# One-hot marks of the expert gates: per-token instructions with scalars in place of broadcast products

## The chip, the cores and the metric

The kernel runs on one core of a Trainium2 chip, as one launch. The metric is the device time of that launch in microseconds (us), here the median of several executions. TensorE multiplies matrices, VectorE (DVE) and ScalarE (ACT) work element by element, GpSimd (POOL) issues the gathers by index, and SyncE (SP) issues most other transfers.

## The reference, cut to what matters

The model is two layers over 512 latent tokens with 256 context tokens before them. Each layer has four token mixers and then a product-key expert layer (PEER), which alone matters here. For every token and each of 8 heads, 16 of the 128 x 128 experts are chosen, so 128 in all; expert (i, j) has a row of the table U and a row of the table V:

```python
top_s, top_j = lax.top_k(cand, PEER_TOPK)
eidx = jnp.take_along_axis(cidx, top_j, axis=-1)
gate = jax.nn.softmax(top_s, axis=-1)
act = jax.nn.gelu(jnp.einsum('td,thkd->thk', xb, u_tab[eidx]).astype(F32))
return jnp.einsum('thk,thkd->td', (gate * act).astype(xb.dtype), v_tab[eidx])
```

## The kernel before, in words

The function `peer` runs once per layer. Most tokens are handled densely: U's products are taken for all 16,384 experts and later multiplied by a gate that is zero wherever a token did not choose the expert. The last tokens (256 in layer 0, 128 in layer 1) gather their chosen rows instead. That leaves 512 dense tokens in layer 0 and 384 in layer 1.

Several streams of work run side by side:

- `s_part` takes U in 128 blocks. ScalarE rounds a block to its high half (`uh`, line 250), VectorE subtracts to get the low half (`ul`, line 251), and TensorE makes 24 long products (`d.S`) from the halves. Both halves have two buffers. `s_ahead(n)` lays n such blocks out at a given place.
- `choose` uses gathered rows on VectorE (lines 1500 and 244, 1024 elements each), copies the next indices (line 1522) and lets GpSimd issue the next gathers (line 1527).
- `route` finds a tile's experts (128 tokens) on VectorE, with long runs of short instructions.
- `build` makes the dense gates of a tile. It transposes the tile's row, column and gate, so that a partition holds one of the 128 choices and the columns are tokens (`ijT`). For a token, a mark for the row is a vector of 128 numbers per choice, one at the row's place and zero elsewhere; likewise for the column. The product of the row marks (weights) with the column marks times the gate, summed over the choices on TensorE, is the 128 x 128 matrix of that token's gates. The gate is split into two fp16 parts, so there are two matmuls per token, into the same PSUM place. ScalarE copies the result out for four tokens at a time.

`build` goes in blocks of 32 tokens: first `s_ahead(5)` in layer 0 or `s_ahead(3)` in layer 1, then twice 16 tokens: marks, `choose` (1 row per block in layer 0, 6 in layer 1), matmuls, copies; then a block goes to DRAM. In layer 0 each block of U also calls `choose` for two rows. The tile framework arranges the instructions of each engine by the order of the program and by what is ready in its planned times, so the streams come out interleaved; each engine then runs its own list in that order.

In the trace, the row marks (`o1`) lie in memory of the residual stream and are named `ro.x`, the column marks are `rt.o`, their products with the gate parts `rt.og`, and the gate matmuls `rt.k<-rt.og,ro.x`. Small helpers record every operation, so many have the helper's line: 236 for a product of two tensors, 240 and 241 for one with scalars, 254 for a matmul.

Before, four tokens at a time lie side by side in `o1`, `o2` and `og` (the innermost step runs over tokens), and a matmul reads every fourth element:

```python
tt(o1, i4, col(0), A.is_equal)
ins = tt(o2, i4, col(1), A.is_equal)
for i in range(2):
    tt(og[:, i], o2, col(2 + i), A.mult)
```

Of the kernel before, what the change touches and what calls it, by code (L numbers as in the profile page):

```python
# [26 lines left out]
# ---------------------------------------------------------------- layout on the host  # L27
# [90 lines left out]
def consts():  # L118
    o = {}
    for n, L in (("l", SEQ), ("c", CTX)):  # L120
        # Half of the times and of the frequencies: e and o below are the sums and differences of the tokens t and
        # their mirror images, of which the even and the odd frequencies need one each for cosine and sine.
        # 0: the filters, t against L - t; 1, 2: tokens, t + 1/2 against L - t - 1/2, and back.
# [91 lines left out]
# ---------------------------------------------------------------- the program  # L215

def body(tc, I, out, dbg=None, stop=None):
# [56 lines left out]
    def segs(n):  # L274
        """columns in PSUM banks: the latents' 512, then the context's 256 before them"""
        return [(max(0, n - 512), n)] + ([(0, n - 512)] if n > 512 else [])

    with pool("keep") as kp, pool("scr", space=DRAM) as dp:
        # ---------------------------------------------------------- persistent
# [13 lines left out]
        def inv_sqrt(o, i, scale, eps_ap_or_val):  # L293
            """(i * scale + eps) ** -0.5"""
            act(o, i, AF.Ln, scale, eps_ap_or_val)
            act(o, o, AF.Exp, -0.5)
# [10 lines left out]
        # ---------------------------------------------------------- modulation vectors  # L307
        def ada(l, rounds, wp, pp, cs, dma, bufs):
            """columns 2048 * r on; the two vectors' products lie on partitions 32 * q and 32 * q + 1"""
# [23 lines left out]
        # ---------------------------------------------------------- Hyena's filters  # L333
        def dft_part(p, n, L, kind, f):
            """two parts each of the cosines and sines of 128 frequencies"""
            t = T(p, [128, 2, 2, L // 2], F32R, "dft", 2)
            G.dma_start(t, I["dft_" + n][:, kind, f])
            if kind < 2:
                t = t.rearrange("p a b (j m) -> p a b j m", m=128)
            return (t[:, 0, 0], t[:, 0, 1]), (t[:, 1, 0], t[:, 1, 1])  # L340

        def sin_(p, t, ps, frq, bias, L):
            """sin(frq * (ps + bias)) with the argument brought to [-pi, pi]"""
# [13 lines left out]
        def spectrum(l, n, L, p, pp, dst_):  # L357
# [12 lines left out]
            # the first half of the times on the upper partitions; the second, mirrored and with the middle in the  # L370
            # place of time L, on the lower ones
# [10 lines left out]
            # forward plus and minus backward, each the sum (0) and difference (1) of a time and its mirror image  # L382
# [34 lines left out]
            # 1 / (L * (sum of the absolute values + EPS)); 1/L = 2/N is the weight of a frequency in the inverse  # L417
# [5 lines left out]
            for f in range(NC):  # L423
# [15 lines left out]
                if f == 0:  # L439
                    # the highest frequency, in the place of the sine of frequency 0  # L440
# [16 lines left out]
        # ---------------------------------------------------------- prologue  # L457
# [18 lines left out]
        # ---------------------------------------------------------- shared pieces  # L476
        def rms_scale(p, pp, srcs, n, tag, tags=(("sq", 2), ("rstd", 1))):
            """1 / sqrt(mean of squares over all rows + EPS), on every partition"""
# [14 lines left out]
        def norm_mod(hps, p, pp, x, l, which, t0, tag, cut=None):  # L493
            """what the products read, in two parts; for the tokens before and from cut on in a pool each"""
# [16 lines left out]
        def projector(wp, pp, src, tag, off=0, ks=range(8), eng=None):  # L511
            """rows of a product with h for the tokens from t0 on, by segments; early(c) fetches a row's weights"""
# [26 lines left out]
        def padded(p, zd, c, tag, bufs, t0):  # L539
            """a row block of z with two zeros before and one behind each stream, in three stretches of 256 tokens"""  # L540
# [12 lines left out]
        def conv(o, xp, taps, bias, t0):  # L553
            """o = sum of w * (token + shift) + bias; the first tap carries the bias"""
# [26 lines left out]
        # ---------------------------------------------------------- RG-LRU  # L581
# [68 lines left out]
        # ---------------------------------------------------------- RWKV-7  # L650
# [5 lines left out]
        def rwkv_prep(l, zd, t0, pp, p):  # L656
            """what the recurrences read, for both tiles of channels; the long parts go through DRAM"""
# [25 lines left out]
            for c in range(2):  # L683
# [6 lines left out]
                # -- decays, keys and the like, channels on partitions  # L690
# [72 lines left out]
                # -- the masked products N whose (1 - N)^-1 each chunk needs; the inverses of their diagonal blocks  # L763
                # of 16, row by row, with a block on each partition
# [27 lines left out]
                # the gate g: what the read-out multiplies by and adds  # L792
# [26 lines left out]
        def rwkv_load(l, st, p):  # L819
            """what all chunks read"""  # L820
# [15 lines left out]
        def rwkv_chain(l, c, t0, stt_, y, p, pp, qp):  # L836
            """the chunks of 128 tokens of one tile of channels, both directions side by side, as generators that can be
            laid out alternately: the inverses of a chunk, and its recurrence"""
# [10 lines left out]
            def inverse(step):  # L849
# [7 lines left out]
                # Wm[d, s]: C against A and R, B against A and R, with the tokens' order as a mask  # L857
# [11 lines left out]
                # XZ[g, d]: the inverse of direction d where g != d, its transpose where g == d  # L869
# [91 lines left out]
        def rwkv_out(l, t0, n, stt_, y, p, pp, tag):  # L961
            """the read-out of the chunks n of both tiles, normed as a group"""
# [34 lines left out]
        def alternate(*gens):  # L997
            """lays the generators' pieces out in turn; (n, g) begins n rounds later"""
# [6 lines left out]
        # ---------------------------------------------------------- mLSTM  # L1005
        def colmajor(ap, t0):
            """the latents' columns of a token row, walked (row, col) where they lie (col, row)"""
            return ap.rearrange("p (c r) -> p r c", r=8)
# [184 lines left out]
        # ---------------------------------------------------------- Hyena  # L1193
        def mix_hyena(l, n, zd, ydst, p, pp):
# [16 lines left out]
            for o in range(2):  # L1211
                # sums (0) and differences (1) of the tokens and their mirror images
# [13 lines left out]
                for f in range(NC):  # L1226
# [9 lines left out]
                    # the sine part of the transform is -q[:, 1]  # L1236
# [12 lines left out]
                # what the tokens and their mirror images have in common (0), and half their difference (1)  # L1249
# [22 lines left out]
        # ---------------------------------------------------------- the four mixers  # L1272
# [6 lines left out]
        def mixers(l, xin):  # L1279
            """xin: (pool, tile) of the residual stream"""  # L1280
# [134 lines left out]
        # ---------------------------------------------------------- PEER  # L1415
        def peer(l, xin):
# [5 lines left out]
            # the last tokens gather the rows that they chose; the others' products go over all rows  # L1422
# [21 lines left out]
            # x waits in DRAM while the routing uses its place  # L1444
# [3 lines left out]
            spare = [xf[:, NE * GB + i * n1:NE * GB + i * n1 + n1].bitcast(F16).rearrange("p (a b c) -> p a b c", a=4, b=128)  # L1448
# [18 lines left out]
            def s_ahead(n):  # L1467
                """U's products, which don't wait for the routing"""
# [9 lines left out]
            def token_rows(t):  # L1478
                """h of a tile of tokens, a token on each partition"""
# [12 lines left out]
            # the last tokens' experts, tile by tile: row e of U, later of V for every token; what has come is used at  # L1492
            # the next calls
# [39 lines left out]
            # ---- routing  # L1533
# [7 lines left out]
            def scores(hc, piece):  # L1541
                """the 16 best keys of half a head for the tokens of a piece"""
# [21 lines left out]
            def route(p, t, io16):  # L1564
                """a tile's experts, of the 16 x 16 pairs of every head the 16 best, and their gates"""
                svh = sv[:, t].rearrange("p (h c) k -> p h c k", c=2)
                # a pair (a, b) with (a + 1)(b + 1) > 16 has 16 before it that are no less: 4 x 16 and 12 x 4 pairs do
# [16 lines left out]
                # the places in the two lists  # L1584
# [13 lines left out]
                # and the keys there  # L1598
# [30 lines left out]
            if CUT[l]:  # L1629
                # the gathered tokens first: their rows come in beside all that follows  # L1630
# [25 lines left out]
            with pool("rg", side=far) as p:  # L1656
                # whole numbers, each four times over: DVE's 2-byte mode needs neighbours in every operand
                iota = T(p, [128, 128, 4], BF, "iota")
                G.dma_start(iota, I["iota"])
                ioth = T(p, [128, 128, 4], F16, "ioth")  # L1660
                V.tensor_copy(ioth, iota)
                i4 = ioth[:, None].broadcast_to((128, 4, 128, 4))
# [3 lines left out]
                def build(t, f):  # L1666
                    """the gates of the tokens of a tile, for all experts"""
# [3 lines left out]
                    # row and column as fp16 whole numbers; the gate, at most 1, times 2^14 as two fp16 parts  # L1671
                    ijT = T(p, [128, 4, 128], F16, "ijT", 2)
                    S.copy(ijT[:, 0:2], ps[:, 0:2])
                    gr = T(p, [128, 128], F32, "gr", 2)
                    act(gr, ps[:, 2], AF.Copy, 2.0 ** 14)
                    V.tensor_copy(ijT[:, 2], gr)
                    tt(ijT[:, 3], gr, ijT[:, 2], A.subtract)
                    for b in range(128 // GB):
# [5 lines left out]
                        for t16 in range(0, GB, 16):  # L1684
                            tk = slice(b * GB + t16, b * GB + t16 + 16)
                            col = lambda i: ijT[:, i, tk].rearrange("p (b t) -> p b t", t=4)[:, :, None].broadcast_to((128, 4, 128, 4))
                            o1 = spare[t16 // 16 % 2]
                            o2 = T(p, [128, 4, 128, 4], F16, "o2", 1)
                            og = T(p, [128, 2, 4, 128, 4], F16, "og", 2)
                            tt(o1, i4, col(0), A.is_equal)  # L1690
                            ins = tt(o2, i4, col(1), A.is_equal)
                            for i in range(2):
                                tt(og[:, i], o2, col(2 + i), A.mult)
# [151 lines left out]
```

## Time and profile before

| | us |
|---|---|
| median of 3 runs | 4990.23 |
| lowest and highest run | 4975.98, 4994.22 |
| profiled execution, span from first to last instruction | 5021.4 |
| TensorE busy in it | 4590.8 |
| VectorE busy in it | 3624.9 |
| ScalarE busy in it | 1777.9 |
| GpSimd busy in it | 1375.8 |

The profile is of one execution; its span stands beside the time of the runs, which are taken without a profile. A busy time is the time in which an engine has an instruction in work, and the start-to-start distance of two instructions can be shorter than the duration of one, since their beginnings and ends overlap. A wait names the instruction that ended last before the waiting one could start.

### The profile page before, as it was taken

The page shows a single profiled execution, that of the slowest core. Times are in us where ns is not written, and L with a number is a line of the kernel's source. Part 1 is how long each engine was busy: PE and PEld are TensorE (multiplying, and loading weights), DVE is VectorE, ACT ScalarE, POOL GpSimd, SP SyncE. Part 2 cuts the span into 40 slices and gives each one's busy share as a digit, 9 for nine tenths or more (in the row PEclk, how much of TensorE's full clock was granted, in tenths as well). Part 3 has the DMA queues.
Part 4 walks back from the last instruction along what each step waited for, and adds up shares of the span by engine and source line. Part 5 has one row for each costly group of instructions (what it writes and reads, how often), then busy time and mean ns, then how long its engine had stood idle before and what let it go on. Part 6 is the DMA issues. An engine that isn't in the chain of part 4 may idle for free. (4 is left out here: it accounts for less than half of the span.)

```text
span 5021.4 us, 66832 instructions
## 1 busy us (share of the span) xinstructions
PE 4590.8 (91%) x24203; PEld 3842.1 (77%) x24203; DVE 3624.9 (72%) x7303; ACT 1777.9 (35%) x2546; POOL 1375.8 (27%) x1117
## 2 busy tenths in 40 slices
PE   7879898799899999799999887898899998999998
PEld 3658567688777888687788665787688898999997
DVE  5772647399788897688889677556589875567777
ACT  4352222353233444322222335212534443333333
POOL 1211111002344454234455222000002332323332
PEclk9889999899999999899999898968999999999999
DMA  4442545346688999899999544203426889888896
GB/s 177 160 137 77 189 161 158 143 130 236 225 298 307 322 329 332 311 352 353 362 379 381 178 152 134 68 19 110 140 80 231 269 284 345 286 283 325 321 328 248
DMA packets 521083, 1170.01 MB, mean 233 GB/s; under 512 B 68192, under 2 KB 250272, under 8 KB 516272
## 3 DMA queue, kind: packets, MB, share of 16 engines
q1 hardware_dynamic: 227440, 563.42, 32.5%
q0 software_dynamic: 134912, 484.06, 27.2%
q10 hardware_dynamic: 158400, 118.25, 7.3%
q8 instruction: 191, 3.13, 0.3%
q14 instruction: 140, 1.15, 0.1%
HBM read 992.95 MB, written 173.02 MB: 232 GB/s over the span
## 5 line engine op out<-in xcount | busy, mean ns | idle before, releaser
L254 PE MATMUL d.S<-mrg.hhi,d.ul 128*128 128x512 f32 (+1 forms) x2048 | 772.6, 377 | 85.4 <-DVE d.ul L251 76.2
L1527 POOL DMA_INDIRECT d.grow<-in_V_dram,d.at x369 | 578.7, 1568 | 712.2 <-DVE d.at L1522 562.4
L254 PE MATMUL d.S<-mrg.hlo,d.uh 128*128 128x512 f32 (+1 forms) x2048 | 760.2, 371 | 0.1
L254 PE MATMUL d.S<-mrg.hhi,d.uh 128*128 128x512 f32 (+1 forms) x2048 | 757.6, 370 | 0.0
L254 PE MATMUL rt.O<-rt.pv,rt.pv 128*128 128x512 f32 (+1 forms) x2580 | 558.6, 366 | 41.5 <-DVE rt.pv L251 41.0
L254 PEld LDWEIGHTS rt.O<-rt.pv,rt.pv 128*128 128x128 f32 x2580 | 468.3, 189 | 108.8 <-issue 48.9
L254 PEld LDWEIGHTS d.S<-mrg.hhi,d.ul 128*128 128x128 f32 x2048 | 398.1, 194 | 144.5 <-DVE d.ul L251 94.7
L247 ACT ACTIVATE d.pa<-d.S 128x512 f32<-128x512 f32 (+1 forms) x256 | 139.7, 546 | 859.3 <-PE d.S L254 794.3
L254 PEld LDWEIGHTS d.S<-mrg.hlo,d.uh 128*128 128x128 f32 x2048 | 397.8, 194 | 39.2 <-DVE mrg.hlo L251 1.2
L254 PEld LDWEIGHTS d.S<-mrg.hhi,d.uh 128*128 128x128 f32 x2048 | 396.1, 193 | 41.4
L1527 POOL DMA_INDIRECT d.grow<-in_Ur_dram,d.at x233 | 302.9, 1300 | 433.2 <-DVE d.at L1522 326.8
L251 DVE TENSOR_TENSOR d.ul<-d.ur,d.uh 128x1024 fp32r<-128x1024 f32 x256 | 311.6, 1219 | 131.0 <-ACT d.uh L250 130.6
L1527 POOL DMA_INDIRECT rt.grow<-in_Ur_dram,rt.at x151 | 228.8, 1515 | 630.1 <-DVE rt.at L1522 569.4
L250 ACT CAST rt.pv<-rt.vr 128x1024 fp32r<-128x1024 f32 x172 | 181.1, 1053 | 588.0 <-DMA rt.vr<-in_V_dram 249.0
L1500 DVE SCALAR_TENSOR_TENSOR d.grow<-d.grow,rt.tok 128x1024 f32<-128x1024 f32 x233 | 281.9, 1221 | 121.6 <-DMA d.grow<-in_Ur_dram,d.at 120.8
L244 DVE SCALAR_TENSOR_TENSOR d.tok<-d.grow,rt.gw,d.tok 128x1024 f32<-128x1024 f32 x245 | 313.7, 1281 | 51.8 <-DMA d.grow<-in_V_dram,d.at 51.5
L254 PE MATMUL d.O<-rt.pv,rt.pv 128*128 128x512 f32 (+1 forms) x1548 | 337.5, 362 | 0.0
L254 PEld LDWEIGHTS d.O<-rt.pv,rt.pv 128*128 128x128 f32 x1548 | 280.7, 188 | 30.2
L254 PE MATMUL rt.O<-d.pv,d.pv 128*128 128x512 f32 (+1 forms) x1260 | 273.1, 365 | 8.1 <-DVE d.pv L251 7.2
L250 ACT CAST d.uh<-d.ur 128x1024 fp32r<-128x1024 f32 x256 | 267.5, 1046 | 27.7 <-issue 11.5
L254 PEld LDWEIGHTS rt.O<-d.pv,d.pv 128*128 128x128 f32 x1260 | 226.8, 188 | 44.1 <-issue 13.6
L254 PE MATMUL z.z<-hhi,z.wlo 128*128 128x512 f32 (+1 forms) x656 | 236.1, 360 | 23.5 <-POOL z.wlo L251 16.3
(619 smaller groups left out, 9380.0 us busy)
## 6 DMA issues: line engine op xcount, KB each, us to landing
d.ur<-in_U_dram SPq DMA_DIRECT2D x256, 512.0 KB, 5.2
rt.vr<-in_V_dram SPq DMA_DIRECT2D x256, 512.0 KB, 6.0
ada.adaw<-in_ada_w_dram POOLq DMA_DIRECT2D x80, 512.0 KB, 4.1
mrg.Ad<-d.pa ACTq DMA_DIRECT2D x128, 256.0 KB, 5.5
rt.gt<-mrg.Gd SPq DMA_DIRECT2D x32, 1024.0 KB, 9.4
rt.ga<-mrg.Ad SPq DMA_DIRECT2D x128, 256.0 KB, 6.9
mrg.Gd<-ro.x ACTq DMA_DIRECT2D x14, 2048.0 KB, 12.1
mrg.Gd<-rt.gst ACTq DMA_DIRECT2D x14, 2048.0 KB, 14.4
```

The lines of the kernel that those rows point to most:

```text
L244: return V.scalar_tensor_tensor(o, a, s, b, op0=op0, op1=op1)
L247: return S.activation(o, i, f, bias=bias, scale=scale)
L250: S.copy(hi, src)
L251: return (eng or V).tensor_tensor(lo, src, hi.bitcast(F32), op=A.subtract)
L254: PE.matmul(ps, l, r, start=start, stop=stop)
L1500: V.scalar_tensor_tensor(g, g, 1.0, s["h"], A.mult, A.mult, accum_out=w[:, e:e + 1])
L1527: G.indirect_dma_start(out=g, out_offset=None, in_=I["Ur"] if r % 256 < 128 else I["V"].rearrange("l j i d -> (l j i) d"), in_offset=bass. ...
```

## The change

For each token, one instruction makes the row marks by comparing 0 to 127 with the token's row, given as a per-partition scalar. Two more compare with the column and multiply by a part of the gate, both as per-partition scalars. The tile `o2` and one of the two buffers of `ijT` go away; `ijT` becomes fp32, as the scalars are read from it; the high part of the gate takes an extra cast. The 128 marks of a token now lie in a row, and the matmuls read them so. (The file's comments are also blanked, which changes no instruction.)

```diff
-            spare = [xf[...].bitcast(F16).rearrange("p (a b c) -> p a b c", a=4, b=128)
+            spare = [xf[...].bitcast(F16).rearrange("p (a b) -> p a b", b=128)
...
-                ioth = T(p, [128, 128, 4], F16, "ioth")
-                V.tensor_copy(ioth, iota)
-                i4 = ioth[:, None].broadcast_to((128, 4, 128, 4))
+                ioth = T(p, [128, 128], F16, "ioth")
+                V.tensor_copy(ioth, iota[:, :, 0])
...
-                    ijT = T(p, [128, 4, 128], F16, "ijT", 2)
+                    ijT = T(p, [128, 4, 128], F32, "ijT", 1)
                     S.copy(ijT[:, 0:2], ps[:, 0:2])
-                    gr = T(p, [128, 128], F32, "gr", 2)
-                    act(gr, ps[:, 2], AF.Copy, 2.0 ** 14)
+                    act(ijT[:, 3], ps[:, 2], AF.Copy, 2.0 ** 14)
+                    gr = T(p, [128, 128], F16, "gr", 2)
+                    V.tensor_copy(gr, ijT[:, 3])
                     V.tensor_copy(ijT[:, 2], gr)
-                    tt(ijT[:, 3], gr, ijT[:, 2], A.subtract)
+                    tt(ijT[:, 3], ijT[:, 3], ijT[:, 2], A.subtract)
...
-                            col = lambda i: ijT[:, i, tk].rearrange("p (b t) -> p b t", t=4)[:, :, None].broadcast_to((128, 4, 128, 4))
                             o1 = spare[t16 // 16 % 2]
-                            o2 = T(p, [128, 4, 128, 4], F16, "o2", 1)
-                            og = T(p, [128, 2, 4, 128, 4], F16, "og", 2)
-                            tt(o1, i4, col(0), A.is_equal)
-                            ins = tt(o2, i4, col(1), A.is_equal)
-                            for i in range(2):
-                                tt(og[:, i], o2, col(2 + i), A.mult)
+                            og = T(p, [128, 16, 2, 128], F16, "og", 2)
+                            for q in range(16):
+                                col = lambda i: ijT[:, i, tk][:, q:q + 1]
+                                ts(o1[:, q], ioth, col(0), None, A.is_equal)
+                                for i in range(2):
+                                    ins = ts(og[:, q, i], ioth, col(1), col(2 + i), A.is_equal, A.mult)
...
-                                        mm(pg[:, q4], o1[:, t4, :, q4], og[:, i, t4, :, q4], i == 1, i == 0)
+                                        mm(pg[:, q4], o1[:, 4 * t4 + q4], og[:, 4 * t4 + q4, i], i == 1, i == 0)
```

## Rows read from the trace of the kernel before

**Rows 1.** The page: its first line, and each engine's busy time.
```profile
span 5021.4 us, 66832 instructions
...
PE 4590.8 (91%) x24203; PEld 3842.1 (77%) x24203; DVE 3624.9 (72%) x7303; ACT 1777.9 (35%) x2546; POOL 1375.8 (27%) x1117
```

**Rows 2.** VectorE's groups by shape: count, busy us, mean ns, idle before.
```profile
L236 DVE TENSOR_TENSOR rt.og<-rt.o,rt.ijT 128x2048 f16<-128x2048 f16 x112 | 133.1, 1217 | 0.1
...
L236 DVE TENSOR_TENSOR ro.x<-rt.ioth,rt.ijT 128x2048 f16<-128x2048 f16 x56 | 68.2, 1218 | 9.5 <-PE rt.k L254 9.5
```

**Rows 3.** Busy time by engine in two stretches, clock, DMA share, GB/s.
```profile
1420.00:2064.00 644.00, 618.18 (x3168) 516.08 (x3166) 549.30 (x850) 273.00 (x323) 294.46 (x194) 0.98 0.92 315
3815.00:4142.00 327.00, 302.21 (x1856) 293.97 (x1855) 268.65 (x397) 157.41 (x191) 109.30 (x69) 0.92 0.84 280
```

**Rows 4.** The same for the gate parts alone: makers (DVE), users (PE).
```profile
1420.00:2064.00 644.00, 127.78 (x1024) 76.00 (x64) 0.98 0.92 315
3815.00:4142.00 327.00, 91.98 (x727) 57.06 (x48) 0.92 0.84 280
```

**Rows 5.** What VectorE waited for, 1420 to 2064: us, times, longest.
```profile
DVE d.ul L251 <- ACT d.uh L250: 30.2, 18, 6.6
DVE d.grow L1500 <- DMA d.grow<-in_Ur_dram,d.at: 26.8, 20, 4.6
DVE d.tok L244 <- DMA d.grow<-in_V_dram,d.at: 21.8, 22, 3.8
```

**Rows 6.** The same from 3815 to 4142.
```profile
DVE d.ul L251 <- ACT d.uh L250: 49.6, 27, 11.1
DVE ro.x L236 <- PE rt.k L254: 8.5, 9, 2.2
```

**Rows 7.** VectorE's timeline (start, us, instruction): a row's and column's marks.
```profile
3843.31 1.22 DVE L236 TENSOR_TENSOR ro.x<-rt.ioth,rt.ijT 128x2048 f16<-128x2048 f16 x1
3844.45 1.22 DVE L236 TENSOR_TENSOR rt.o<-rt.ioth,rt.ijT 128x2048 f16<-128x2048 f16 x1
```

**Rows 8.** The same timeline: 128 two-byte elements and a constant, twice.
```profile
1112.22 0.19 DVE L240 TENSOR_SCALAR rt.pf<-rt.pf 128x128 bf16<-128x128 bf16 x1
1112.33 0.49 DVE L1597 COPY_PREDICATED rt.pf<-rt.over,rt.pf 128x128 bf16<-128x128 uint8 x2
...
3952.54 0.18 DVE L240 TENSOR_SCALAR rt.pf<-rt.pf 128x128 bf16<-128x128 bf16 x1
3952.64 0.48 DVE L1597 COPY_PREDICATED rt.pf<-rt.over,rt.pf 128x128 bf16<-128x128 uint8 x2
```

**Rows 9.** The same: 128 fp32 elements, one per-partition scalar, and the next.
```profile
369.45 0.28 DVE L240 TENSOR_SCALAR rw.fs<-lru.sig,rp.fm 128x128 f32<-128x128 f32 x1
369.64 0.68 DVE L236 TENSOR_TENSOR rw.Wm<-rw.r,lru.msk 128x512 f32<-128x512 f32 x1
```

**Rows 10.** The same: two per-partition scalars at 184.86, constants at 186.64.
```profile
184.86 0.67 DVE L241 TENSOR_SCALAR rp.kd<-rp.ra,rp.rwpar 128x768 f32<-128x768 f32 x1
185.45 0.41 DVE L737 TENSOR_TENSOR_SCAN rp.cum<-cst,rp.lw__234_1169 128x128 f32<-128x128 f32 x1
...
186.64 0.55 DVE L241 TENSOR_SCALAR rp.ra<-rp.ra 128x768 f32<-128x768 f32 x1
187.11 1.68 DVE L737 TENSOR_TENSOR_SCAN rp.cum<-cst,rp.lw__234_1169 128x128 f32<-128x128 f32 x5
```

**Rows 11.** Instructions on rt.ijT: ns min/median/max, first and last start.
```profile
L1673 ACT CAST rt.ijT<-rt.k x7: 363/365/376, 1419.7 to 4046.8; 128x256 f16<-128x256 f32 x7
...
L236 DVE TENSOR_TENSOR rt.ijT<-rt.gr,rt.ijT x7: 277/281/284, 1423.2 to 4049.5; 128x128 f16<-128x128 f32 x7
```

**Rows 12.** TensorE's timeline: long products of 384 columns.
```profile
3842.82 0.33 PE L254 MATMUL d.S<-mrg.hhi,d.uh 128*128 128x384 f32 x1
...
3843.34 0.33 PE L254 MATMUL d.S<-mrg.hhi,d.uh 128*128 128x384 f32 x1
```

**Rows 13.** Line 240: ns min/median/max, first and last start.
```profile
L240 DVE TENSOR_SCALAR rt.pf<-rt.pf x10: 178/184/383, 1112.2 to 3952.5; 128x128 bf16<-128x128 bf16 x10
```

More of the change, by code (lines that the diff above doesn't have):

```diff
@@ L1447, in peer @@
             n1 = 4 * 128 * 4 // 2
-            spare = [xf[:, NE * GB + i * n1:NE * GB + i * n1 + n1].bitcast(F16).rearrange("p (a b c) -> p a b c", a=4, b=128)
+            spare = [xf[:, NE * GB + i * n1:NE * GB + i * n1 + n1].bitcast(F16).rearrange("p (a b) -> p a b", b=128)
                      for i in range(2)]
```

## The prediction

> **What bounds the kernel now.** I read the page first, for the shares of the engines over the span [rows 1]: TensorE is busy 91% and VectorE 72%. An average like this decides nothing for a change that touches one stage, so the second view is the list of VectorE's groups by line and shape. It shows what the marks are now: large fp16 tensor_tensors of 2048 elements, four for each 16 tokens, and 56 times 16 tokens in all [rows 2].
>
> The third view is the busy time of the engines in the two stretches in which the marks are made [rows 3]. In layer 0 (1420 to 2064 us) VectorE is busy 549.3 of 644 us and TensorE 618.2; in layer 1 (3815 to 4142 us) it is 268.7 and 302.2 of 327 us. The reader is to see that TensorE leads in both, and that VectorE has only 94.7 and 58.4 us free. The same windows for the gate parts alone give the split of the work: 64 of their instructions in layer 0 and 48 in layer 1, which is 32 and 24 times 16 tokens [rows 4].
>
> The fourth view says what VectorE's free time is made of. In layer 0, 30.2 us of it wait for ScalarE's rounded half of a U block (ScalarE there waits for TensorE to give a buffer back), and most of the rest for gathered rows to land [rows 5]. In layer 1, 49.6 us are of the first kind and 8.5 us wait for TensorE to free a mark buffer [rows 6]. So VectorE is second in both stretches by a small margin; in some stalls it is TensorE that waits for it.
>
> **What the change removes.** Four tensor_tensors for each 16 tokens. Each lasts 1.22 us, but the next begins before it ends: from start to start it is 1.14 us [rows 7]. So 4 x 1.14 = 4.56 us go.
>
> **What it adds.** For each token one tensor_scalar of 128 fp16 elements with one per-partition scalar, and two with two of them: 48 instructions for 16 tokens. No row has this form, so I build it from three neighbours, always from start to start.
> - A tensor_scalar of 128 two-byte elements with a constant is followed after 0.11 and 0.10 us, 0.105 in the mean [rows 8].
> - What a per-partition scalar costs: over 768 fp32 elements, the form with two of them is followed after 0.59 us, the one with constants after 0.47 us [rows 10]. That is 0.12 us for two, 0.06 for one.
> - A check: 128 fp32 elements with one per-partition scalar are followed after 0.19 us [rows 9]; fp32 streams more slowly, so this lies above 0.105 + 0.06 = 0.165, as it should.
>
> So the row's mark costs 0.165 us, a column mark with its gate part 0.105 + 0.12 = 0.225 us, a token 0.165 + 2 x 0.225 = 0.615 us, and 16 tokens 9.84 us. The change adds 9.84 - 4.56 = 5.28 us of VectorE for each 16 tokens: 169 us in layer 0 (32 times), 127 us in layer 1 (24 times), 296 us together. The ends: if the scalars cost nothing, 48 x 0.105 = 5.04 us and +0.48 (27 us in all); if fp16 ran only like the fp32 row, 0.19 and 0.25 us, then 11.04 us and +6.48 (363 us). I take 5.28, because its nearest rows have the element size and, apart, the scalars.
>
> **Where it lands.** VectorE would need 549.3 + 169 = 718 us in a stretch of 644, and 268.7 + 127 = 396 in one of 327. Cover for it is only the free time, so at least 74 and 69 us stick out, 143 together, and at most all 296. VectorE becomes the bound of both stretches. What stands behind the marks on its queue is the U blocks' low halves, which TensorE's long products wait for, and the gathered rows' products, after which the next gather is issued; all of them are late by as much. The products after the marks' stretch start when the gates are done, and none of the later work is moved into it. Of the free time I count as used up only the waits for ScalarE's half, 30.2 + 49.6 = 80 us: they come from TensorE holding a buffer, and end once VectorE is the late one. The waits for gathered rows stay, as the gathers are issued from the same queue of steps. That gives 296 - 80 = +216 us.
>
> **Small parts.** The row, column and gate tile becomes fp32 with one buffer in place of two. So the copies of the next tile of tokens wait for the last marks of the one before. From the first of these copies to the end of the last is 4 us (1419.7 to 1423.2 + 0.28) in layer 0 [rows 11]; at the five changes of tile that is 0 to 20 us, and I take 0, since routing, U blocks and gathered rows stand ready for VectorE there. The extra cast per tile is one of 7. The matmuls now read their marks in a row instead of every fourth element. 1,751 of the 1,792 fall into the two windows and keep TensorE 127.8 + 92.0 us, some 0.125 us each [rows 4]. The long products move 384 columns every 0.173 us (three steps in 0.52 us), 0.058 us per 128 [rows 12]. So the layout may give between 0 and 1,792 x 0.067 = 120 us of TensorE. On the path I take 0, because TensorE no longer ends these stretches.
>
> **The sum.** The profiled execution spans 5021.4 us; the median of the runs is 4990.2, 0.6% less. 5021 + 216 = 5237 us for a profiled span, and at the same ratio (0.9938) 5205 us for the median. The bounds +143 and +296 give 5132 and 5284.
>
> **Rivals.**
> - *The scalars are fetched behind the instruction before, so they cost nothing.* Then the marks cost +27 us of VectorE in all, and 80 us of waits cover it: 4990 us, no change. [...] Against this rival stand the 0.59 beside 0.47 us [rows 10] and the 0.19 us [rows 9]: two forms and both above the constant's. Chance 0.04.
> - *TensorE stays the bound and gains from marks in a row.* This is the one on the faster side. It decides if a token's marks take less than 0.285 us (now, 4.56 / 16) plus the free time per token, 94.7 / 512 = 0.185 us in layer 0 and 58.4 / 384 = 0.152 in layer 1: below some 0.44 us. Then the matmuls' gain counts, up to 120 us: (5021 - 120) x 0.9938 = 4871, and 4930 for half of it. For it speaks that TensorE is at 96% and 92% in the windows [rows 3]; against it that 0.44 us needs scalars at a third of what rows 10 show. Chance 0.04.
> - *GpSimd and the marks get in each other's way.* The short form with a constant took 0.383 us once of 10 times, against a median of 0.184 [rows 13], 0.2 us more. GpSimd has 194 and 69 instructions in the two windows, mostly gathers [rows 3]. At 0.2 us each that is 53 us more: 5257 us, and 5290 with 30 us more of new waits. [...] Chance 0.12.
> - *fp16 streams no faster than fp32.* +363 - 80 = +283: 5272 us. Against it: 0.105 beside 0.19 us [rows 8, 9]. Chance 0.06.
>
> **Chances and range.** My forecast of 5205, with its own bounds 5132 to 5284, has 0.74. A measurement of this kernel tells about 0.5%, 25 us, from no change. Faster has the second rival's 0.04, same the first one's 0.04, and slower the rest, 0.92. The range leaves out the two small rivals below, goes a little under the lower bound for what TensorE may give back in waits, and takes in the last two above: 5115 to 5300.
>
> **What the profile after would show.** VectorE some 2,460 instructions more; 896 marks of a row and 1,792 of column and gate, in long runs spaced 0.16 and 0.22 us; VectorE near 95% in both stretches, the waits for ScalarE's half gone, and TensorE's waits for the U blocks' low halves grown to over 100 us. The two stretches some 120 and 95 us longer, all others as before. The forecast is wrong if the marks are spaced 0.11 us, if VectorE keeps idle time in both stretches, or if the time goes up outside of them.

## The result and the profile after

The changed kernel takes 5201.1 us in the median of 4 runs (5181.19 to 5246.79), against 4991.93 for the kernel before in the same comparison: a ratio of 1.0455, 95% interval 1.0398 to 1.0512. The forecast was 5205. The profiled execution spans 5245.0 us, 223.6 more than the one before [rows 1]. Executions come in two kinds here, some 50 us apart by layer 1's mixers (last section): the profiled ones before and after are both of the longer kind, and a median can mix the two.

The page of the kernel after, its span and shares of the engines:

```profile
span 5245.0 us, 69339 instructions
...
PE 4617.5 (88%) x24203; PEld 3805.9 (73%) x24203; DVE 3909.6 (75%) x9774; ACT 1768.8 (34%) x2546; POOL 1285.5 (25%) x1117
```

VectorE has 2,471 instructions and 284.7 us more. The groups of VectorE by line and shape show the marks:

```profile
L241 DVE TENSOR_SCALAR rt.og<-rt.ioth,rt.ijT 128x128 f16<-128x128 f16 x1792 | 483.0, 318 | 0.0
L240 DVE TENSOR_SCALAR ro.x<-rt.ioth,rt.ijT 128x128 f16<-128x128 f16 x896 | 232.5, 260 | 2.3 <-ACT rt.ijT L1671 2.3
```

These durations overlap, so the price is read from VectorE's timeline, from one row mark to the next (a line "x2" is a pair):

```profile
1541.58 0.25 DVE L240 TENSOR_SCALAR ro.x<-rt.ioth,rt.ijT 128x128 f16<-128x128 f16 x1
1541.75 0.53 DVE L241 TENSOR_SCALAR rt.og<-rt.ioth,rt.ijT 128x128 f16<-128x128 f16 x2
1542.19 0.24 DVE L240 TENSOR_SCALAR ro.x<-rt.ioth,rt.ijT 128x128 f16<-128x128 f16 x1
...
1544.63 0.24 DVE L240 TENSOR_SCALAR ro.x<-rt.ioth,rt.ijT 128x128 f16<-128x128 f16 x1
```

The row mark takes 0.17 us until the next begins, the pair 0.44. Five tokens take 3.05 us, so a token 0.61 us and 16 tokens 9.76, against 4.56 before [rows 7]: 5.20 us more, times 56 is 291 us.

Busy time in the two stretches of the marks, with columns as in [rows 3]:

```profile
1420.00:2232.00 812.00, 647.56 (x3152) 498.11 (x3150) 706.28 (x2245) 266.37 (x319) 237.32 (x192) 0.86 0.73 252
3970.00:4385.00 415.00, 310.43 (x1922) 280.56 (x1920) 390.92 (x1454) 163.06 (x200) 77.11 (x69) 0.81 0.69 232
```

VectorE now leads in both, with 105.7 us free in layer 0 and 24.1 in layer 1; in layer 0 the DMA share fell from 0.92 to 0.73. What VectorE waits for in layer 0 (us, times, longest; gathered rows are named `rt.grow` or `d.grow` by the section in which they were fetched):

```profile
DVE d.tok L244 <- DMA rt.grow<-in_V_dram,rt.at: 63.1, 9, 7.8
DVE rt.grow L1500 <- DMA rt.grow<-in_Ur_dram,rt.at: 33.7, 5, 6.9
DVE d.grow L1500 <- DMA d.grow<-in_Ur_dram,d.at: 5.6, 5, 1.6
...
DVE d.tok L244 <- DMA d.grow<-in_V_dram,d.at: 1.4, 2, 0.8
```

Before the change the rows named `rt.grow` had little part in these waits:

```profile
DVE rt.grow L1500 <- DMA rt.grow<-in_Ur_dram,rt.at: 2.9, 3, 1.9
DVE d.tok L244 <- DMA rt.grow<-in_V_dram,rt.at: 2.3, 1, 2.3
```

And TensorE, there too:

```profile
PE d.S L254 <- DVE d.ul L251: 86.3, 34, 6.3
PE rt.k L254 <- DVE rt.og L241: 53.5, 197, 2.6
```

Against [rows 5] the wait for ScalarE's half is gone, and the products' waits for gathered rows nearly doubled: from 53.8 us (26.8 and 21.8 [rows 5], 2.9 and 2.3) to 103.8. In layer 1 the wait for ScalarE's half fell from 49.6 us [rows 6] to this:

```profile
DVE d.ul L251 <- ACT d.uh L250: 21.5, 14, 4.5
```

TensorE's granted clock is lower too: 0.86 and 0.81 in the two stretches, 0.98 and 0.92 before [rows 3]. That is not what lengthened them: in layer 0 no wait of VectorE for TensorE shows, and a run below that gives TensorE more to do in both stretches leaves both as long.

Where the 223.6 us are: VectorE's first product with the gates (`rt.gm`) marks the end of layer 0's stretch. It starts at 2250.1 us in place of 2087.3: +163. From x being loaded in layer 1 (`ro.x<-xd`) to its last reload behind the marks (`ro.x<-mrg.xs`) it takes 709.4 us in place of 634.7: +75. All the rest together is 14 us shorter.

### The profile page after: what moved, and what is told of

Same layout as the page of the kernel before. It is cut to its first block, busy times and chain, and to the rows that moved or that the text cites. A ratio compares the mean times of both kernels' runs of the same rounds, so it can differ in the third digit from the quotient of the medians.

```text
span 5245.0 us, 69339 instructions
## 1 busy us (share of the span) xinstructions
PE 4617.5 (88%) x24203; PEld 3805.9 (73%) x24203; DVE 3909.6 (75%) x9774; ACT 1768.8 (34%) x2546; POOL 1285.5 (25%) x1117
## 5 line engine op out<-in xcount | busy, mean ns | idle before, releaser
L254 PE MATMUL d.S<-mrg.hhi,d.ul 128*128 128x512 f32 (+1 forms) x2048 | 791.4, 386 | 181.5 <-DVE d.ul L251 172.8
L254 PE MATMUL d.S<-mrg.hlo,d.uh 128*128 128x512 f32 (+1 forms) x2048 | 777.5, 380 | 0.1
L254 PE MATMUL d.S<-mrg.hhi,d.uh 128*128 128x512 f32 (+1 forms) x2048 | 773.7, 378 | 0.0
L1527 POOL DMA_INDIRECT d.grow<-in_V_dram,d.at x369 | 539.3, 1462 | 741.1 <-DVE d.at L1522 507.7
L241 DVE TENSOR_SCALAR rt.og<-rt.ioth,rt.ijT 128x128 f16<-128x128 f16 x1792 | 483.0, 318 | 0.0
L254 PEld LDWEIGHTS d.S<-mrg.hlo,d.uh 128*128 128x128 f32 x2048 | 409.3, 200 | 42.0 <-DVE mrg.hlo L251 0.9
L1527 POOL DMA_INDIRECT rt.grow<-in_Ur_dram,rt.at x151 | 196.5, 1302 | 795.1 <-DVE rt.at L1522 431.4
L1527 POOL DMA_INDIRECT d.grow<-in_Ur_dram,d.at x233 | 282.6, 1213 | 438.5 <-DVE d.at L1522 290.9
L251 DVE TENSOR_TENSOR d.ul<-d.ur,d.uh 128x1024 fp32r<-128x1024 f32 x256 | 310.4, 1217 | 47.5 <-ACT d.uh L250 47.3
L254 PE MATMUL rt.k<-rt.og,ro.x 128*128 128x128 f16 x1792 | 197.7, 241 | 133.7 <-DVE rt.og L241 88.6
L254 PEld LDWEIGHTS <-ro.x 128*128 128x128 f16 x1792 | 129.0, 100 | 201.1 <-issue 146.3
```

The costliest lines, as they stand in the source:

```text
L241: return V.tensor_scalar(o, a, s1, s2, op0=op0, op1=op1)
L251: return (eng or V).tensor_tensor(lo, src, hi.bitcast(F32), op=A.subtract)
L254: PE.matmul(ps, l, r, start=start, stop=stop)
L1527: G.indirect_dma_start(out=g, out_offset=None, in_=I["Ur"] if r % 256 < 128 else I["V"].rearrange("l j i d -> (l j i) d"), in_offset=bass. ...
```

## The experiments

The first column of numbers is 16 tokens' marks on VectorE, from start to start in the traces. "L0" is the start of layer 0's first gate product, "L1" the stage of layer 1 just named; both from the profiled execution. The median is of all runs of the kernel, the ratio against the runs of before that belong to them. Three executions of the changed kernel whose VectorE runs one and the same list (after, and the two small edits at the end) have L0 between 2244.0 and 2252.5 us and L1 between 706.7 and 709.4; a difference of a few us between two rows is no more than that.

| kernel | marks of 16 tokens, us | L0 | L1 | median | ratio to before, 95% |
|---|---|---|---|---|---|
| before | 4.56 | 2087.3 | 634.7 | 4992 | |
| after | 9.76 | 2250.1 | 709.4 | 5201 | 1.0455 [1.0398, 1.0512] |
| constants | 4.90 | 2100.9 | 637.3 | 4981 | 1.0031 [0.9990, 1.0072] |
| one scalar each | 7.80 | 2178.4 | 666.4 | 5114 | 1.0282 [1.0209, 1.0355] |
| after, every fourth read | 9.76 | 2245.0 | 709.5 | 5222 | 1.0483 [1.0435, 1.0531] |
| before, read in a row | 4.56 | 2078.4 | 624.0 | 4991 | 1.0013 [0.9977, 1.0050] |
| pairs | 4.56 | 2082.3 | 621.1 | 4976 | 0.9999 [0.9958, 1.0041] |
| three products, in a row | 3.42 | 2084.7 | 631.5 | 4964 | 0.9979 [0.9936, 1.0021] |
| pairs, half of U's loads | 4.56 | 2061.7 | 609.7 | 4925 | 0.9899 [0.9847, 0.9950] |
| pairs, ScalarE's part | 3.42 | 2113.5 | 689.9 | 5083 | 1.0167 [1.0110, 1.0224] |

**Constants for the scalars.** The changed kernel with its 48 instructions per 16 tokens:

```diff
-ts(o1[:, q], ioth, col(0), None, A.is_equal)
+ts(o1[:, q], ior, 5.0, None, A.is_equal)
-ins = ts(og[:, q, i], ioth, col(1), col(2 + i), A.is_equal, A.mult)
+ins = ts(og[:, q, i], ior, 9.0, 0.5, A.is_equal, A.mult)
```

> The changed kernel with the same 48 mark instructions per 16 tokens, but every scalar a constant (the compared stream is a tile of row numbers, so that the marks still wait for the routing; the gates are then wrong, and nothing else is left out). Theory (the per-partition scalars are the price): a mark is followed after 0.105 us instead of 0.165 and 0.22, 16 tokens take 5.0 us instead of 9.75, VectorE's load is that of before within 30 us, and with the matmuls reading in a row the time is 4900 to 5000 us. Rival (short instructions as such are the price, by their number or by how the planner lays them out): the time stays at 5150 us or more.

VectorE's timeline in this run:

```profile
1545.10 0.19 DVE L240 TENSOR_SCALAR ro.x<-rt.ior 128x128 f16<-128x128 f16 x1
1545.20 0.29 DVE L241 TENSOR_SCALAR rt.og<-rt.ior 128x128 f16<-128x128 f16 x2
1545.40 0.19 DVE L240 TENSOR_SCALAR ro.x<-rt.ior 128x128 f16<-128x128 f16 x1
```

Every mark is followed after 0.10 us, one constant or two, and 16 tokens take 4.90 us. So neither the number of the instructions nor their length is the price of the marks on VectorE. The time is in the theory's range, and the rival's 5150 is out. The medians agree with before (4981 beside 4982), but the stages are not quite the same: L0 and L1 together are 16 us longer than before, and some 35 us longer than with either of the kernels below that also read in a row (2078.4 and 624.0 us, 2082.3 and 621.1). That is more than the 19 us of marks; the rest isn't explained. The framework arranges VectorE's list anew for each kernel, and the order of its other instructions differs here in part.

**One per-partition scalar each.**

```diff
-ins = ts(og[:, q, i], ioth, col(1), col(2 + i), A.is_equal, A.mult)
+ins = ts(og[:, q, i], ioth, col(1), None, A.is_equal)
```

> The changed kernel with 48 short instructions per 16 tokens, each with one per-partition scalar: the column marks compare only, so the gate parts are left out. Theory (each per-partition scalar costs some 0.06 us of VectorE from start to start, and VectorE's list sets both stretches): a mark every 0.165 us, 16 tokens 7.9 us, 1.9 us less than with two scalars, times 56 some 105 us less than the changed kernel: 5080 to 5120 us. Rival A (the first scalar has all the price, the second is free): marks stay at 0.22 us and the time at 5200. Rival B (the time has a threshold and not a slope, VectorE sets the end only when it is over-full): close to the kernel before, 4990 to 5040 us.

```profile
1566.79 0.25 DVE L240 TENSOR_SCALAR ro.x<-rt.ioth,rt.ijT 128x128 f16<-128x128 f16 x1
1566.95 0.41 DVE L240 TENSOR_SCALAR rt.og<-rt.ioth,rt.ijT 128x128 f16<-128x128 f16 x2
1567.28 0.25 DVE L240 TENSOR_SCALAR ro.x<-rt.ioth,rt.ijT 128x128 f16<-128x128 f16 x1
```

On VectorE's timeline a token takes 0.488 us (four in 1.95), a mark 0.163. So the steps are 0.10 us with constants, 0.163 with one per-partition scalar, 0.22 with two: 0.06 us for each. The time, 5114 us, is in the theory's range; both rivals (5200, and 4990 to 5040) are out. VectorE's other instructions come in almost the same order as in the changed kernel, so that this pair of runs differs in little but the scalars: 110 us less of marks, and L0 and L1 together 115 us shorter.

**The matmuls' reading apart from the marks.** Once the changed kernel with operands of every fourth element, as before; once the kernel before with operands in a row:

```diff
-mm(pg[:, q4], o1[:, 4 * t4 + q4], og[:, 4 * t4 + q4, i], i == 1, i == 0)
+mm(pg[:, q4], o1v[:, t4, :, q4], ogv[:, t4, i, :, q4], i == 1, i == 0)
```

> The changed kernel, its marks as they are, but the matmuls read every fourth element of the marks of four tokens, as before (the gates are then wrong). Theory (VectorE ends both stretches, TensorE has room): a pair of weights and matmul goes from 0.056 back to some 0.117 us in a burst, 110 us of TensorE in all, and the time stays within 25 us of the changed kernel's 5201. Rival (TensorE still shares in the bound, the row layout has already paid back a part): 5250 to 5310 us.

```diff
-mm(pg[:, q4], o1[:, t4, :, q4], og[:, i, t4, :, q4], i == 1, i == 0)
+mm(pg[:, q4], o1v[:, t4, 128 * q4:128 * q4 + 128], ogv[:, i, t4, 128 * q4:128 * q4 + 128], i == 1, i == 0)
```

> The kernel before, its four large products as they are, but the matmuls read 128 neighbouring elements of the marks (the gates are then wrong). Theory (TensorE led both stretches of the kernel before by a small margin, VectorE is close behind): the gate matmuls fall from 0.117 to 0.056 us, 110 us of TensorE, and some half of it reaches the end before VectorE takes over: 4900 to 4960 us. Rival (VectorE was the bound already): 4980 to 5000 us, no change.

The reading has its price on TensorE. Two bursts of 24 gate matmuls on its timeline, the first before the change, the second after:

```profile
3846.12 3.00 PE L254 MATMUL rt.k<-rt.og,ro.x 128*128 128x128 f16 x24
```

```profile
3983.79 1.51 PE L254 MATMUL rt.k<-rt.og,ro.x 128*128 128x128 f16 x24
```

That is 0.125 us each by this reading, and 0.063 in a row. But neither run moved the time: 5222 beside 5201 with overlapping intervals, as the theory of the first had it, and 4991 beside 4982. In the first, TensorE's busy time on the gate products rose from 197.7 to 234.2 us (1,791 of the 1,792), and L0 and L1 stayed. The second is the telling one. Busy time of the gate parts alone in its stretches, makers and users as in [rows 4]:

```profile
1420.00:2055.00 635.00, 76.15 (x1024) 75.96 (x64) 0.96 0.93 319
3798.00:4123.00 325.00, 56.06 (x766) 57.03 (x48) 0.92 0.86 292
```

TensorE lost 52 and 36 us of work against [rows 4], and the stages only 9 and 11, in one profiled execution each. Theory and its 4900 to 4960 us missed, and the rival's time held; its reason, that VectorE was the bound, is tested below. TensorE's wait for U's low halves in layer 0 grew from 21.6 to 39.2 us.

**Marks in a row by tensor_tensors.** Each row, column and gate value is kept twice, and the innermost step runs over two neighbouring experts of one token; all of the computation is there.

```diff
-col = lambda i: ijT[:, i, tk].rearrange("p (b t) -> p b t", t=4)[:, :, None].broadcast_to((128, 4, 128, 4))
+col = lambda i: ijT[:, i, tk][:, :, None].broadcast_to((128, 16, 64, 2))
```

> The full computation with the marks of a token in a row, made by the four large products of before: row, column and gate parts are kept twice side by side, so that the innermost step of every operand runs over two neighbours. Theory: the products keep 1.14 us from start to start, the matmuls take 0.056 us in a burst, and the time is that of the kernel before with row reads, 4900 to 4960 us. [...]

```profile
L236 DVE TENSOR_TENSOR rt.og<-rt.o,rt.ijT 128x2048 f16<-128x2048 f16 x112 | 132.6, 1216 | 0.1
```

The products kept their rate (1217 ns before [rows 2]), the matmuls read in a row, and the time stayed: 0.9999, and 4976 us, above the theory's 4900 to 4960. So the layout is to be had without the scalars, and is worth nothing measurable here.

**Less work on VectorE.** If VectorE's list with its waits had been the bound before, 64 us less of it must show. The pairs, without the product for the low gate part:

```diff
-for i in range(2):
-    tt(og[:, i], o2, col(2 + i), A.mult)
+tt(og[:, 0], o2, col(2), A.mult)
```

> The kernel before with marks in a row by four tensor_tensors (each value kept twice), of which the one for the low gate part is left out; the products read the high part twice. It takes 56 x 1.14 = 64 us from VectorE, 36 in layer 0 and 27 in layer 1, beside some 85 us from TensorE through the row. Theory (VectorE's list with its waits sets both stretches already before the change): some 35 to 60 us less than with four tensor_tensors, 4910 to 4950 us. Rival (neither engine sets layer 0's stretch but the gathered rows and U's transfers, at 92% of the DMA engines): layer 0's stretch stays within 10 us, and only layer 1's falls, 15 to 27 us: 4950 to 4975 us.

It gave 4990.5 us, 0.9989 [0.9953, 1.0025]: neither range. In its profiled execution (8616 us) the matmuls were far slower throughout, with 675 to 678 ns for a long product of 512 columns against 394 to 402 before, so its rows answer nothing. A second execution, at 19072 us, was no better:

> The run with the low gate part left out once more, for its profile, as the time had not fallen (4990 us). What is open is where 64 us less of VectorE went. If the gathered rows and U's transfers set layer 0's stretch, its first gate product starts within 10 us of the one with all four tensor_tensors (2082 us), with VectorE's waits for gathered rows and for ScalarE's half grown by 30 us or more, and only layer 1's stage is shorter (621 us before, 595 to 615 then). If VectorE's list set both, the first gate product starts 20 us or more earlier, and the time comes back outside of the stretches.

Then the same cut in the kernel before, its operands read as they lie:

> The kernel before with its own marks, of which the low gate part is left out, and products that read neighbours as they lie (another pairing of marks and gates): 64 us less of VectorE and some 85 us less of TensorE in the two stretches, as in the run that gave 4990 us. What is open is where they went. Halving U's loads has taken 21 us from layer 0's stretch and 12 us from layer 1's stage, so the transfers have a share in the floor. If VectorE's list still counts below that, the first gate product starts 20 us or more before 2078 us and layer 1's stage falls below 610 us, with a time of 4920 to 4960 us; the 4990 us are then the layer-1 mixers' spread. If not, both stay within 10 us of the run with four tensor_tensors read in a row (2078 and 624 us), VectorE's waits grow by what it saved, and the time is 4970 to 5000 us.

Busy time in layer 0's stretch:

```profile
1420.00:2040.00 620.00, 564.58 (x3037) 457.17 (x3036) 507.72 (x809) 252.72 (x307) 289.36 (x193) 0.97 0.94 322
```

VectorE's largest wait there, and the one in layer 1's stretch:

```profile
DVE d.ul L251 <- ACT d.uh L250: 63.6, 26, 7.1
...
DVE d.ul L251 <- ACT d.uh L250: 75.3, 24, 12.2
```

VectorE has 112 us free in 620. Against the same kernel with all four products (before, read in a row), L0 came 6 us later and L1 is 7.5 us longer; VectorE's wait for ScalarE's half in layer 0 was this there:

```profile
DVE d.ul L251 <- ACT d.uh L250: 24.7, 14, 8.8
```

So it grew by 39 us, about as much as was saved (32 x 1.14 = 36). The time, 4964 us, is a little under the floor reading's 4970 to 5000, but not by more than its interval. So neither VectorE nor TensorE alone set the end of these stretches before the change. The order of VectorE's list differs in part here too; what that took or gave isn't separated.

**Half of U's loads.** The pairs, with every block loaded used twice:

```diff
-ur = T(up, [128, 8, 128], F32, "ur", URB[l])
-SP.dma_start(ur, I["U"][l, j])
+if j % 2 == 0:
+    had[0] = T(up, [128, 8, 128], F32, "ur", URB[l])
+    SP.dma_start(had[0], I["U"][l, j])
+ur = had[0]
```

> Marks in a row by four tensor_tensors, and only every other block of U is loaded; the one loaded is used for two blocks, so the output is that of another U. Nothing changes on the engines: each block is still split and multiplied. It takes 23 MB of layer 0's 214 MB in the stretch, at 314 GB/s some 70 us of transfer. Theory (the transfers, 92% busy, are the floor of layer 0's stretch): its first gate product starts 30 to 70 us earlier than 2082 us, and the time falls to 4890 to 4945 us. Rival (the steps on the engines set it, each waiting for the other in a fixed order, and the transfers only fill the room): within 10 us of 2082, and 4960 to 4990 us.

Busy time in layer 0's stretch:

```profile
1420.00:2040.00 620.00, 566.15 (x3145) 460.54 (x3145) 543.91 (x841) 265.27 (x320) 301.10 (x192) 0.98 0.88 288
```

L0 is 20.6 us earlier than with the pairs and L1 11.4 us shorter. That is the largest gain of any cut on the side of the kernel before. The time, 4925 us, is in the theory's range, but L0 moved by less than its 30 to 70, and the DMA share only fell from 0.92 to 0.88. The transfers have a share in the floor; they aren't all of it.

**The low gate part on ScalarE.** All of the computation, in search of a faster version:

```diff
-for i in range(2):
-    tt(og[:, i], o2, col(2 + i), A.mult)
+tt(og[:, 0], o2, col(2), A.mult)
+for q in range(16):
+    act(og[:, 1, q], o2[:, q], AF.Copy, glo[:, b * GB + t16 + q:b * GB + t16 + q + 1])
```

> All of the computation, marks in a row by three tensor_tensors on VectorE, and the low gate part token by token on ScalarE with the gate as a per-partition scale: 16 short activations in place of one tensor_tensor. Theory (VectorE's list sets both stretches, and ScalarE, 41% busy in layer 0's, has room for 16 x 0.2 to 0.3 us more per 16 tokens): 4920 to 4960 us. Rival A (the transfers set layer 0): 4960 to 4985 us. Rival B (ScalarE's short activations delay its rounded halves and the eviction of the gate products, in order on its queue): 5020 us or more.

ScalarE's timeline:

```profile
1605.86 3.33 ACT L247 ACTIVATE rt.og<-rt.o,rt.glo 128x128 f16<-128x128 f16 x11
```

VectorE's largest wait in either layer's stretch:

```profile
DVE d.ul L251 <- ACT d.uh L250: 99.2, 32, 7.5
...
DVE d.ul L251 <- ACT d.uh L250: 96.7, 26, 9.9
```

At 0.30 us each the activations stand ahead of the rounded halves on ScalarE's queue, and VectorE waits for those 99 and 97 us. Rival B held: +1.7%. ScalarE was busy only 60% of layer 0's stretch (401.9 of 670 us); it is the order on its queue that costs.

**Two small edits of the changed kernel.** The index copies and gathers ordered behind the first token's marks:

```diff
-ins = ts(og[:, q, i], ioth, col(1), col(2 + i), A.is_equal, A.mult)
+o = ts(og[:, q, i], ioth, col(1), col(2 + i), A.is_equal, A.mult)
+ins = o if q == 0 and i == 0 else ins
```

> The changed kernel, all of it, but the index copies and the issue of gathers that follow each 16 tokens' marks are ordered behind the first token's marks in place of the last one's. Theory (in layer 0 the gathers are issued later by the marks' longer run, and so the waits for gathered rows doubled from 52 to 104 us): these waits fall back by 30 to 50 us and the time to 5150 to 5180 us. Rival (the rows are late because the whole list is longer, wherever the issue stands): waits of some 100 us and 5200 us, within 25.

5238 us, 1.0482 [1.0424, 1.0539], L0 at 2252.5 us and L1 709.4, and waits for gathered rows as after (63.1 and 34.1 us for the two largest). But VectorE's and GpSimd's instructions came out in the same order, so the run is a repetition and tells nothing of the anchor.

Two buffers for the tile of rows, columns and gates (`"ijT", 2`):

> The changed kernel, all of it, with two buffers for the tile of rows, columns and gates. Prediction's step (the one buffer costs 0 to 20 us at the five changes of tile, taken as 0): 5190 to 5215 us. Rival (each change waits for all of the tile before, 4 us): 20 us less, 5170 to 5190 us.

5224 us, 1.0522 [1.0414, 1.0629], above both ranges; L0 at 2244.0 us and L1 706.7, 6 and 3 us less than after. The one buffer costs next to nothing.

## Why the prediction was right

**The price of the marks** was the term that carried the sum, and it was built from neighbours. Predicted 0.165 us, 0.225 us and 9.84 us for 16 tokens; measured 0.17, 0.22 and 9.76. The constants and the single scalars show the cause: the per-partition scalars have 4.86 of the 5.20 us that 16 tokens cost more, at 0.06 us each, and 221 of the 238 us in L0 and L1; the short instructions as such have 0.34 us. The rival "scalars are fetched for nothing" is out: a mark is followed after 0.10 us with constants, 0.163 with one scalar and 0.22 with two. That fp32 streams more slowly, as the check by [rows 9] has it, shows on larger instructions of the kernel before: a tensor_tensor takes 1219 ns for 1024 fp32 elements (`d.ul`) and 1217 ns for 2048 fp16 elements [rows 2].

**Where it lands.** Predicted +216 us, measured +223.6 between the spans and +209 between the medians. The two larger doses bear out the form of the argument, that what VectorE gets beyond the waits that it replaces sets the end: against the kernel before, single scalars add 181 us of marks and L0 and L1 together 123, two scalars add 291 and give 238. So 53 to 58 us are absorbed, and from the one dose to the other the stages follow one for one. The smallest dose does not fit: the constants add 19 us (56 x 0.34), which the free time should have taken, and L0 and L1 grew by 16. That the median came within 4 us of the forecast is in part luck. The four runs lie 66 us apart, the profiled execution before is longer than any timed run of that kernel (4930 to 5020 us), and the two stages' terms were off, as follows.

**The split over the stages was off.** With 169 us and 30 absorbed layer 0 should have grown by 139, and layer 1 by 127 less 50, 77; the text's own "some 120 and 95" does not follow from these terms. Measured were 163 and 75, of 166 and 125 us of marks. The step that failed in layer 0 is "the waits for gathered rows stay": they grew by 50 us, so that VectorE is 87% busy there and not "near 95%" (94% in layer 1 is right). GpSimd's waits for the index copies that precede a gather rose there from 218 to 294 us, in a stretch 168 us longer; whether moving these copies ahead would bring the rows sooner stays open, since the one attempt left their order as it was. The wait for ScalarE's half vanished in layer 0, as predicted, and in layer 1 only fell to 21.5. All the rest of the kernel, taken as unchanged, came out 14 us shorter.

**"TensorE leads in both, VectorE second by a small margin"** described busy shares, and as a bound it was wrong. Cutting TensorE by 88 us in the two stretches took 20 from the stages and nothing from the median, and cutting VectorE by 64 as well gave nothing further. The transfers, at 92%, have a part in the floor: halving U's loads took 32 us from the stages. That the rest is hand-offs between TensorE, ScalarE's halves and VectorE fits the waits that grew with the cuts of TensorE and of VectorE, but no run shows it. For the forecast it did not matter, since the change pushed VectorE far beyond all of them.

**The small parts.** The one buffer was taken as 0 and is. The layout was given 0 to 120 us of TensorE and taken as 0 on the path. In bursts it is worth 1,792 x 0.062 = 111 us; in TensorE's busy time on the gate products it was 93 us in the kernel before (225.1 to 132.5) and 27 in the changed one (197.7), where they come few at a time as the marks get ready. On the path it was worth nothing measurable in either. The rival "TensorE gains" fell with the token's 0.61 us, above its 0.44 (which needs scalars at 0.4 of what rows 10 show, not "a third"). GpSimd's contention isn't seen as a bound: the means of the marks lie 10 and 12 ns above their medians (318 beside 308, 260 beside 248), some 28 us over all 2,688, and VectorE's busy time rose by 284.7 us in all, no more than the 291 that the uncontested steps add up to. TensorE's waits for U's low halves came to 86.3 and 48.7 us, not "over 100" in each stretch but 135 together.

## What to carry to other kernels

Price a short instruction from start to start, and price its per-partition scalars apart from its elements: here they about doubled the marks' time (9.76 against 4.90 us). When a change adds much to an engine that is second by a little, the added time less the waits that it replaces was a good forecast here, once one asks of each wait whether it goes, stays or grows. When a change takes work away, busy shares don't tell what it brings: TensorE, VectorE and the transfers lay so close together here (96%, 85% and 92% of layer 0's stretch [rows 3]) that no cut of one brought its own size. An engine with much free time was no place for work here, as what others wait for stands behind it on its queue: with the low gate part ScalarE was busy only 60% of layer 0's stretch, and the kernel took 1.7% longer.

## What the runs showed of the hardware

- A tensor_scalar of 128 fp16 elements is followed after 0.10 us with constants, 0.163 with one per-partition scalar, 0.22 with two.
- A pair of weight load and matmul of 128 x 128 fp16 takes 0.125 us in a burst if its operands lie in every fourth element, and 0.063 in a row (24 of them in 3.00 and in 1.51 us).
- A tensor_tensor of 2048 fp16 elements keeps its rate when the innermost step has only two elements (1216 ns against 1217 with four).
- TensorE's granted clock in layer 1's mixers differs between executions, whatever the kernel. These mixers took 694 to 702 us in seven of the profiled executions and 647 to 653 in five. Busy time and granted clock there, before the change and then with the pairs:

```profile
3290.00:3320.00 30.00, 28.30 (x237) 24.65 (x235) 18.83 (x49) 8.95 (x37) 0.00 (x0) 0.92 0.20 59
3320.00:3350.00 30.00, 30.00 (x136) 24.93 (x136) 12.76 (x44) 3.24 (x10) 0.00 (x0) 0.50 0.00 1
3380.00:3410.00 30.00, 30.00 (x132) 26.46 (x132) 9.20 (x29) 4.80 (x13) 0.00 (x0) 0.50 0.00 1
```

```profile
3284.00:3314.00 30.00, 28.31 (x238) 24.28 (x238) 17.55 (x55) 9.21 (x35) 0.00 (x0) 0.94 0.10 31
3314.00:3344.00 30.00, 30.00 (x237) 24.96 (x237) 23.16 (x70) 5.90 (x19) 0.00 (x0) 1.00 0.01 2
```

The work ahead is the same (28.3 of 30 us busy). Then the granted clock is at 0.50 for 90 us in the one and at 1.00 in the other, and TensorE does 136 matmuls in 30 us in place of 237. In the 120 us from 480 us after x is stored, the mean granted clock is 0.59 in all seven with 694 to 702 us and 0.93 to 0.97 in the five with 647 to 653. That is some 50 us, 1% of the kernel, and why stages were compared here and not spans alone.
